# mLSTM heads: the denominator's squares bounded row by row, one column sum per token tile in place of two

## The chip, the cores and the metric

The kernel runs on one core of one Trainium2 chip. The metric is the device time of one execution in microseconds (us). Times in the profile are in us from the start of the profiled span, unless marked ns.

## The reference

The program is a two-layer streaming encoder on 512 tokens of width 1024 in float32. The change touches one part of layer 0: the four mLSTM heads of width 192 (DH).

```
num = sum_s s[t,s] v[s] + inter * q_t C          # per head, 192 values for each token
den = sum_s s[t,s]      + inter * q_t . n
h   = num / max(|den|, exp(-m_t))
h   = h * rsqrt(mean(h*h) + EPS)                  # over the 192 values of the head
out = h * head_g * sigmoid(o)                     # goes to the output projection
```

The division and the norm together are one factor for each token and head: `num * rsqrt(mean(num^2) + EPS * max(den^2, exp(-2 m)))`. Both kernels compute that factor.

## The kernel before, in words

**Layout.** Activations lie transposed: features on the 128 partitions, the 512 tokens along the free dimension. Most products are made of three single-precision products of rounded parts (`mm3`, lines 175 to 177: high x high, low x high, high x low), so each float32 operand is first split: ScalarE casts the high part (line 136), VectorE subtracts to get the low part (line 137). The weights take this path too (`wr` raw, `wh` high, `wl` low, three buffers each). The text calls one `mm3` of 512 columns a triple of filler.

**A head.** A head of 192 features fills one full tile (`full`) and half of a second (`sh`, rows `rs`). `mlstm_head` goes over four blocks of 128 source tokens: `weighted_scores` makes the decayed scores (a product with `sel` at line 1155 spreads a row of gates, ScalarE takes the exponential at line 1157, GpSimd masks it at line 1159, VectorE multiplies it with the scores at line 1168), and `products` multiplies them with the values into two accumulators, `nums`. The first accumulator holds 128 of the head's 192 numerators. The second holds the other 64 in half of its rows; in the other half the value matrix is all ones, so that all 64 rows hold the denominator.

**The end of a head.** ScalarE squares both accumulators (line 1195) and VectorE multiplies them into the output gate `og` (line 1197). For each of four tiles of 128 tokens TensorE then multiplies the squares, as the stationary operand, with a constant `mcf` of two columns (lines 1202 and 1203): column 0 gathers the numerators' sum of squares, column 1 the mean of the 64 denominator rows. On 128x4 values VectorE takes the maximum with `floor2`, which is exp(-2m) with tokens on the partitions (line 1207), scales it, adds the mean of squares, and takes an inverse square root by three Newton steps (lines 222 to 228). `diagonal` makes two diagonal matrices of the result (line 237), `spread` multiplies them with ones (line 250), so that each token's factor stands in all rows, and line 1216 multiplies `og` by it. The result is split and becomes an operand of the output projection.

**The gate work.** `gate_rows` computes the gates on four rows (one for each head) of 512 tokens. Its row `mr` is m, bounded at line 1086. Eight small transposes (lines 1096 and 1097) turn two rows into columns; of the second ScalarE takes exp(-2x) into `floor2` (line 1099).

**Order.** `weave(job, filler, each)` runs a job and takes `each` steps of filler at every `yield` of the job, or `each * n` at `yield n`; a filler step is mostly one `mm3` of a projection. In this part of the program a scheduler then orders the instructions of each engine by its own estimates and assigns the buffers; each engine executes its instructions in that order. Accumulators come in three kinds: `mm` (three banks), `sc` (three) and `tr` (two). The head's last factor is needed by the output projection: `outp.part(0, 4, 5)` and `outp.part(1, 4, 5)` follow the last head with no other work between.

Of the kernel before, what the change touches and what calls it, by code (L numbers as in the profile page):

```python
# [21 lines left out]
MEM = 256  # L22
AW = 768
AH = 4
DH = AW // AH
BH = 12
HD = 64
# [3 lines left out]
EPS = 1e-6  # L31
# [19 lines left out]
def f(ap):  # L51
    return ap.bitcast(F32)
# [3 lines left out]
def trunk(  # L56
# [18 lines left out]
    nc = tc.nc  # L75
    V, A, G = nc.vector, nc.scalar, nc.gpsimd

    cpool = ctx.enter_context(tc.tile_pool(name="cpool", bufs=1))
# [6 lines left out]
    dram = ctx.enter_context(tc.tile_pool(name="dram", bufs=1, space=bass.MemoryType.DRAM))  # L85

    def sb(tag, shape, dtype=F32):
        count[0] += 1
        return pool.tile(shape, dtype, tag=tag, name=f"{tag}{count[0]}", bufs=bufs[tag])

    def ps(tag):
        count[0] += 1
        return psum.tile([P, S], F32, tag=tag, name=f"p{tag}{count[0]}", bufs=pbufs[tag])

    def small(n=4):
        return sb("s", [P, 32])[:, :n]


    ident = cpool.tile([P, P], F32, name="ident")
    make_identity(nc, ident)  # L100
    ones = cpool.tile([P, P], F32, name="ones")
# [7 lines left out]
        out=maskf, in_=maskf, pattern=[[1, P]], base=0, channel_multiplier=-1,  # L109
# [8 lines left out]
            V.tensor_copy(sel[q], ident[q, 32 * s : 32 * s + AH].unsqueeze(2).to_broadcast([AH, AH, P]))  # L118
    eps = cpool.tile([P, 1], F32, name="eps")
    V.memset(eps, EPS)  # L120

    mcf = cpool.tile([P, 3, 2], F32, name="mcf")
    V.memset(mcf, 0.0)
    V.memset(mcf[:, 0, 0:1], 1.0)
    V.memset(mcf[:HD, 1, 0:1], 1.0)
    V.memset(mcf[HD:, 1, 1:2], 1.0 / HD)
    V.memset(mcf[:HD, 2, 1:2], 1.0 / HD)
    V.memset(mcf[HD:, 2, 0:1], 1.0)


    HEADS = (slice(0, HD), slice(HD, P))

# [86 lines left out]
    def rsqrt(y, v):  # L219
        n = v.shape[-1]  # L220
        yi = y.bitcast(I32)
        V.tensor_scalar(yi, v.bitcast(I32), 1, None, op0=ALU.logical_shift_right)
        V.tensor_scalar(yi, yi, -1, 0x5F3759DF, op0=ALU.mult, op1=ALU.add)
        t = small(n)
        for _ in range(3):
            V.tensor_mul(t, y, y)
            V.scalar_tensor_tensor(t, t, -0.5, v, op0=ALU.mult, op1=ALU.mult)
            V.scalar_tensor_tensor(y, t, 1.5, y, op0=ALU.add, op1=ALU.mult)
# [17 lines left out]
    def spread(dgs, tag):  # L246

        o = ps(tag)
        for i, dg in enumerate(dgs):
            nc.tensor.matmul(o, onesr, dg, start=i == 0, stop=i == 1)  # L250
        return o
# [176 lines left out]
    with tc.manual_schedule(engines={mybir.EngineType.PE, mybir.EngineType.Activation, mybir.EngineType.DVE}):  # L428
# [9 lines left out]
        for q in range(KT // 2 + 1):  # L438
            if q < KT // 2:
                tp = ps(("tr", "sc")[q % 2])  # L440
# [577 lines left out]
    e, u, c, r = (cpool.tile([P, TT, AH], F32, name=f"gate{i}") for i in range(4))  # L1018
    tot = cpool.tile([AH, 16], F32, name="tot")
    acol = cpool.tile([P, TT, AH], F32, name="acol")  # L1020
    floor2 = cpool.tile([P, TT, AH], F32, name="floor2")
    RO = [0, 512, 896, 1152, 1280]

    rp = []
# [1 line left out]
    def gate_rows():  # L1026

        V.tensor_copy(ic, gt[:, :, :AH])
        V.scalar_tensor_tensor(e, fg, -1.0, fg, op0=ALU.mult, op1=ALU.min)
        A.activation(e, e, AF.Exp)  # L1030
        V.tensor_scalar(u, e, 1.0, None, op0=ALU.add)
        A.activation(lf, u, AF.Ln)
        V.scalar_tensor_tensor(c, u, -1.0, e, op0=ALU.add, op1=ALU.subtract)
        V.reciprocal(r, u)
        yield
        pin(V.tensor_mul(c, c, r))
        V.tensor_tensor(out=lf, in0=lf, in1=c, op=ALU.subtract)
        V.scalar_tensor_tensor(lf, fg, 0.0, lf, op0=ALU.min, op1=ALU.subtract)
        yield
        yield  # L1040
        lfp, icp = ps("tr"), ps("tr")
        for T in range(TT):
            nc.tensor.transpose(lfp[:AH, T * P : (T + 1) * P], lf[:, T, :], ident)
            nc.tensor.transpose(icp[:AH, T * P : (T + 1) * P], ic[:, T, :], ident)
        yield
        lfr, br, ar, mr = (sb("t", [P, S])[:AH, :] for _ in range(4))
        rr = [sb("t", [P, S]) for _ in range(2)]
        rp.extend(sb("u", [P, S], F32R) for _ in range(2))
        for t in rp:
            G.memset(f(t), 0.0)  # L1050
        pin(V.tensor_copy(lfr, lfp[:AH, :]))
        yield
        for T in range(TT):
            sl = slice(T * P, (T + 1) * P)
            pin(V.tensor_tensor_scan(br[:, sl], ones[:AH, :], lfr[:, sl], 0.0, ALU.mult, ALU.add))
        yield
        pin(V.tensor_tensor(out=ar, in0=icp[:AH, :], in1=br, op=ALU.subtract))
        yield
        carry = 0.0
        for T in range(TT):  # L1060
            sl = slice(T * P, (T + 1) * P)
            pin(V.tensor_tensor_scan(mr[:, sl], ar[:, sl], ar[:, sl], carry, ALU.max, ALU.max))
            if T < TT - 1:
                e_ = (T + 1) * P - 1
                V.tensor_tensor(out=tot[:, T : T + 1], in0=mr[:, e_ : e_ + 1], in1=br[:, e_ : e_ + 1], op=ALU.add)
                carry = tot[:, T : T + 1]
            yield
        for s in range(TT):
            off = None
            for T in range(s, TT):  # L1070
                sl = slice(T * P, (T + 1) * P)
                dst = rr[s // 2][64 * (s % 2) : 64 * (s % 2) + AH, sl]
                if T == s:
                    pin(V.tensor_scalar(dst, mr[:, sl], -1.0, None, op0=ALU.mult))
                else:
                    end = br[:, T * P - 1 : T * P]
                    if off is None:
                        off = end
                    else:
                        k = 4 + 4 * s + T - s  # L1080
                        V.tensor_tensor(out=tot[:, k : k + 1], in0=off, in1=end, op=ALU.add)
                        off = tot[:, k : k + 1]
                    V.tensor_scalar(dst, mr[:, sl], -1.0, off, op0=ALU.mult, op1=ALU.add)
            yield
        pin(V.tensor_tensor(out=mr, in0=mr, in1=br, op=ALU.add))
        V.tensor_scalar(mr, mr, -40.0, None, op0=ALU.max)
        yield
        for s in range(TT):
            q, t = 64 * (s % 2), rp[s // 2]
            src, hi = rr[s // 2][q : q + AH, s * P :], t[q : q + AH, s * P :]  # L1090
            pin(V.tensor_copy(hi, src))
            V.tensor_tensor(out=t[q + 32 : q + 32 + AH, s * P :], in0=src, in1=f(hi), op=ALU.subtract)
            yield
        tp = ps("tr")
        for T in range(TT):
            nc.tensor.transpose(tp[:, T * AH : (T + 1) * AH], ar[:, T * P : (T + 1) * P], ident[:AH, :AH])
            nc.tensor.transpose(tp[:, 16 + T * AH : 16 + (T + 1) * AH], mr[:, T * P : (T + 1) * P], ident[:AH, :AH])
        pin(V.tensor_copy(acol, tp[:, :16].rearrange("p (t h) -> p t h", t=TT)))
        A.activation(floor2, tp[:, 16:32].rearrange("p (t h) -> p t h", t=TT), AF.Exp, scale=-2.0)

    mixes = [None] * KT

# [41 lines left out]
    def mlstm_head(h):  # L1144
        hp, odd = divmod(h, 2)
# [46 lines left out]
        sqs = []  # L1192
        for o, j, r in ((nums[0], full, slice(0, P)), (nums[1], sh, rs)):
            sq = sb("t", [P, S])
            A.activation(sq, o, AF.Square)
            sqs.append(sq)
            V.tensor_tensor(out=og[j][r, :], in0=o[r, :], in1=og[j][r, :], op=ALU.mult)
        yield
        st = ps("sc")
        for T in range(TT):  # L1200
            sl = slice(T * P, (T + 1) * P)
            nc.tensor.matmul(st[:, 2 * T : 2 * T + 2], sqs[0][:, sl], mcf[:, 0, :], start=True, stop=False)
            nc.tensor.matmul(st[:, 2 * T : 2 * T + 2], sqs[1][:, sl], mcf[:, 1 + odd, :], start=False, stop=True)
            yield 0.581
        st = st[:, : 2 * TT].rearrange("p (t c) -> p t c", c=2)
        z, fc = small(), small()
        V.tensor_tensor(out=z, in0=st[:, :, 1], in1=floor2[:, :, h], op=ALU.max)
        V.tensor_scalar(z, z, EPS, 1e-35, op0=ALU.mult, op1=ALU.max)
        V.scalar_tensor_tensor(z, st[:, :, 0], 1.0 / DH, z, op0=ALU.mult, op1=ALU.add)
        rsqrt(fc, z)  # L1210
        dg = diagonal(fc)
        yield 2.673
        fb = spread(dg, "sc")
        yield
        for j, r in ((full, slice(0, P)), (sh, rs)):
# [12 lines left out]
    fill = chain(a_tiles(2), a_memory_queries(0), a_tiles(3, 4), a_tiles(5), a_memory_queries(1))  # L1228
    memkv = load_memory_kv(0)
    weave(mlstm_head(0), fill, 1.4)  # L1230
    until(lambda: og[2] is not None, fill)
    weave(mlstm_head(1), fill, 1.125)
# [292 lines left out]
```

## Time and profile before

| what | value |
|---|---|
| time, median of 3 runs | 1197.71 us (1197.57 to 1198.04) |
| span of the profiled execution | 1197.4 us |
| TensorE products busy | 1186.5 us, 99% |
| TensorE weight loads busy | 1039.1 us, 87% |
| VectorE busy | 967.3 us, 81% |
| ScalarE busy | 718.4 us, 60% |
| GpSimd busy | 123.3 us, 10% |

The page gives the span of the profiled execution, 1197.4 us, and no time of its own around it; the median of the timed runs is 0.3 us above. In the rows, PE is TensorE, PEld its weight loads, DVE VectorE, ACT ScalarE, POOL GpSimd, SP SyncE. A row of the timeline reads: start, length, engine, line, operation, tile written from tiles read, shapes, number of merged instructions, and in brackets the idle time before it and what ended that. Products on TensorE are pipelined, so their lengths overlap: the distance of two starts is what a product costs. A float32 product (not split) is recorded as two passes.

### The profile page before, as it was taken

The page shows a single profiled execution, that of the slowest core. Times are in us where ns is not written, and L with a number is a line of the kernel's source. Part 1 is how long each engine was busy: PE and PEld are TensorE (multiplying, and loading weights), DVE is VectorE, ACT ScalarE, POOL GpSimd, SP SyncE. Part 2 cuts the span into 40 slices and gives each one's busy share as a digit, 9 for nine tenths or more (in the row PEclk, how much of TensorE's full clock was granted, in tenths as well). Part 3 has the DMA queues.
Part 4 walks back from the last instruction along what each step waited for, and adds up shares of the span by engine and source line. Part 5 has one row for each costly group of instructions (what it writes and reads, how often), then busy time and mean ns, then how long its engine had stood idle before and what let it go on. Part 6 is the DMA issues. An engine that isn't in the chain of part 4 may idle for free.

```text
span 1197.4 us, 18206 instructions
## 1 busy us (share of the span) xinstructions
PE 1186.5 (99%) x6735; PEld 1039.1 (87%) x6735; DVE 967.3 (81%) x1772; ACT 718.4 (60%) x1290; POOL 123.3 (10%) x206
## 2 busy tenths in 40 slices
PE   9999999999999999999999999999999999999997
PEld 8988888888889989999888888888889988999986
DVE  6778688878978888888698888997897888888855
ACT  5646577655655555555575667776565655555545
POOL 1200101000021111111021000001001011011100
PEclk9999999999999999999999999999999999999999
DMA  8634111454266666665563223146336466665551
GB/s 283 212 92 123 54 54 57 134 152 133 88 157 162 153 162 155 151 144 129 152 189 120 89 71 99 55 130 201 116 89 150 110 138 141 141 141 136 121 158 71
DMA packets 199131, 155.97 MB, mean 130 GB/s; under 512 B 7976, under 2 KB 179458, under 8 KB 199042
## 3 DMA queue, kind: packets, MB, share of 16 engines
q1 hardware_dynamic: 183906, 119.74, 34.2%
q0 software_dynamic: 14560, 34.02, 13.7%
q8 instruction: 53, 0.87, 0.3%
q10 hardware_dynamic: 576, 1.05, 0.2%
q14 instruction: 36, 0.29, 0.1%
HBM read 126.27 MB, written 32.44 MB: 133 GB/s over the span
## 4 chain that ended last, share of the span: by engine, by line
PE 93%; DMA 2%; ACT 2%; DVE 2%; issue 0%; SPq 0%; ACTq 0%; DVEq 0%
PE pmm L175 15%; PE pmm L176 15%; PE pmm L177 15%; PE ptr L175 6%; PE ptr L177 6%; PE ptr L176 6%; PE pmm L791 6%; PE psc L177 5%; PE psc L175 5%; PE psc L176 5%; PE pmm L790 3%; PE psc L525 2%; DMA wr<-in_mem_w_kv_dram 2%; PE ptr L1352 1%; PE ptr L1373 1%; PE ptr L1374 1%
## 5 line engine op out<-in xcount | busy, mean ns | idle before, releaser
L175 PE MATMUL pmm<-u,wh 128*128 128x512 f32 (+1 forms) x872 | 309.1, 355 | 0.3 <-ACT u L136 0.2
L176 PE MATMUL pmm<-u,wh 128*128 128x512 f32 (+1 forms) x872 | 306.3, 351 | 0.0
L177 PE MATMUL pmm<-u,wl 128*128 128x512 f32 (+1 forms) x872 | 306.3, 352 | 0.0
L137 DVE TENSOR_TENSOR wl<-wr,wh 128x1024 fp32r<-128x1024 f32 (+3 forms) x172 | 199.8, 1163 | 55.1 <-ACT wh L136 53.1
L136 ACT CAST wh<-wr 128x1024 fp32r<-128x1024 f32 (+3 forms) x172 | 172.1, 1002 | 99.8 <-PE pmm L176 45.2
L177 PEld LDWEIGHTS pmm<-u,wl 128*128 128x128 f32 x872 | 164.5, 189 | 20.9
L175 PEld LDWEIGHTS pmm<-u,wh 128*128 128x128 f32 x872 | 164.5, 189 | 18.7 <-ACT u L136 1.1
L176 PEld LDWEIGHTS pmm<-u,wh 128*128 128x128 f32 x872 | 164.7, 189 | 18.3 <-DVE u L137 0.5
L175 PE MATMUL ptr<-u,wh 128*128 128x512 f32 x272 | 106.7, 392 | 0.0
L177 PE MATMUL ptr<-u,wl 128*128 128x512 f32 x272 | 106.1, 390 | 0.0
L176 PE MATMUL ptr<-u,wh 128*128 128x512 f32 x272 | 105.9, 389 | 0.0
L759 POOL DMA_DIRECT2D xspill<-t x64 | 55.5, 867 | 462.5 <-ACT t L758 457.1
L136 ACT CAST u<-pt 128x512 fp32r<-128x512 f32 x102 | 62.8, 618 | 47.2 <-DVE pt L881 47.1
L137 DVE TENSOR_TENSOR u<-pt,u 128x512 fp32r<-128x512 f32 x102 | 69.9, 689 | 11.2 <-ACT u L136 8.5
L175 PE MATMUL psc<-u,wh 128*128 128x256 f32 (+1 forms) x232 | 76.1, 328 | 0.0
L177 PE MATMUL psc<-u,wl 128*128 128x256 f32 (+1 forms) x232 | 75.9, 327 | 0.0
L176 PE MATMUL psc<-u,wh 128*128 128x256 f32 (+1 forms) x232 | 75.9, 327 | 0.0
L791 PE MATMUL pmm<-u,u 128*128 128x512 f32 x192 | 69.6, 397 | 0.0
L943 ACT ACTIVATE t<-t 128x512 f32<-128x512 f32 x34 | 21.5, 632 | 79.4 <-DVE t L666 79.4
L827 DVE TENSOR_TENSOR t<-t,pmm 128x256 f32<-128x256 f32 x72 | 30.2, 420 | 45.0 <-ACT t L825 45.0
L758 ACT COPY t<-ptr 128x512 f32<-128x512 f32 x64 | 37.4, 584 | 42.8 <-PE ptr L177 42.8
L666 DVE SCALAR_TENSOR_TENSOR t<-t,cols,t 128x511 f32<-128x511 f32 x80 | 59.6, 746 | 3.7 <-ACT t L673 3.7
(305 smaller groups left out, 2671.5 us busy)
## 6 DMA issues: line engine op xcount, KB each, us to landing
wr<-in_ffn_w_up_dram SPq DMA_DIRECT2D x54, 512.0 KB, 4.5
wr<-in_ffn_w_down_dram SPq DMA_DIRECT2D x38, 512.0 KB, 4.1
pt<-in_ffn_w_up_dram SPq DMA_DIRECT2D x34, 512.0 KB, 6.0
xspill<-t POOLq DMA_DIRECT2D x64, 256.0 KB, 5.2
wr<-in_a_w_in_dram SPq DMA_DIRECT2D x20, 512.0 KB, 3.7
xspill<-u POOLq DMA_DIRECT2D x32, 256.0 KB, 2.7
u<-xspill SPq DMA_DIRECT2D x32, 256.0 KB, 5.1
wr<-in_w_kv_dram SPq DMA_DIRECT2D x12, 512.0 KB, 3.8
```

Of the source, the lines that this page charges most:

```text
L136: high = A.copy(hi, src) if on_act else V.tensor_copy(hi, src)
L137: low = V.tensor_tensor(out=lo, in0=src, in1=f(hi), op=ALU.subtract)
L175: nc.tensor.matmul(o, lh, rh, start=first, stop=False, skip_group_check=more)
L176: nc.tensor.matmul(o, lh, rl, start=False, stop=False, skip_group_check=more)
L177: nc.tensor.matmul(o, ll, rh, start=False, stop=last, skip_group_check=more)
L525: nc.tensor.matmul(o, a, b, start=first and i == 0, stop=i == 1)
L666: V.scalar_tensor_tensor(acc[:, n:], src[:, : S - n], self.fw[:, c * FT + j : c * FT + j + 1], acc[:, n:], op0=ALU.mult, op1=ALU.add,)
L758: A.copy(t, o)
L759: G.dma_start(xspill[j], t, accum_op=ALU.add)
L790: nc.tensor.matmul(r[:, :H], w[1][:, k], p[i - 1][:, :H], start=False, stop=False, skip_group_check=True)
L791: nc.tensor.matmul(r, w[0][:, k], p[i - 1], start=False, stop=k == n - 1, skip_group_check=True)
L827: V.tensor_tensor(out=o, in0=o, in1=r[:, H:], op=ALU.add)
```

## The change

The squares of the denominator are bounded where they lie. VectorE replaces the 64 denominator rows of the second tile of squares by max(den^2 * c, floor) with c = EPS * DH / HD, then adds the two tiles of squares. One float32 product for each tile of tokens, with a single column of ones, sums the 128 rows of the result: that is DH times what stands under the root. `mcf` and its memsets go, as do the second product, the maximum and the scaling behind the sums.

For this the floor is needed on 64 rows for each head, with tokens along the free dimension. `gate_rows` takes the exponential on the row `mr` itself, scales and bounds it, writes it to DRAM with one DMA and reads it back with four broadcasting DMAs, all on GpSimd's queue, into two tiles of the kind `bias`, one for each pair of heads. Four of the eight small transposes go. The yields around the sums change: 2.4 ahead of them and 3.4 behind them, in place of 0.581 after each pair and 2.673 behind.

```diff
-    mcf = cpool.tile([P, 3, 2], F32, name="mcf")
-    V.memset(mcf, 0.0)
-    ...
-    floor2 = cpool.tile([P, TT, AH], F32, name="floor2")
+    floor2 = dram.tile([AH, S], F32, name="floor2")
+    floors = []
...
         V.tensor_scalar(mr, mr, -40.0, None, op0=ALU.max)
+        A.activation(mr, mr, AF.Exp, scale=-2.0)
+        V.tensor_scalar(mr, mr, EPS * DH / HD, 1e-35, op0=ALU.mult, op1=ALU.max)
+        G.dma_start(floor2, mr)
+        for hp in range(2):
+            floors.append(sb("bias", [P, S]))
+            for odd, half in enumerate(reversed(HEADS)):
+                row = floor2[2 * hp + odd]
+                src = bass.AP(tensor=row.tensor, offset=row.offset, ap=[[0, HD], [1, S]])
+                G.dma_start(floors[hp][half, :], src)
         yield
...
-            nc.tensor.transpose(tp[:, 16 + T * AH : 16 + (T + 1) * AH], mr[:, T * P : (T + 1) * P], ident[:AH, :AH])
...
-        A.activation(floor2, tp[:, 16:32].rearrange("p (t h) -> p t h", t=TT), AF.Exp, scale=-2.0)
...
             V.tensor_tensor(out=og[j][r, :], in0=o[r, :], in1=og[j][r, :], op=ALU.mult)
+        dr = HEADS[1 - odd]
+        V.scalar_tensor_tensor(
+            sqs[1][dr, :], sqs[1][dr, :], EPS * DH / HD, floors[hp][dr, :], op0=ALU.mult, op1=ALU.max
+        )
+        V.tensor_add(sqs[0], sqs[0], sqs[1])
         yield
+        yield 2.4
         st = ps("sc")
         for T in range(TT):
-            sl = slice(T * P, (T + 1) * P)
-            nc.tensor.matmul(st[:, 2 * T : 2 * T + 2], sqs[0][:, sl], mcf[:, 0, :], start=True, stop=False)
-            nc.tensor.matmul(st[:, 2 * T : 2 * T + 2], sqs[1][:, sl], mcf[:, 1 + odd, :], start=False, stop=True)
-            yield 0.581
-        st = st[:, : 2 * TT].rearrange("p (t c) -> p t c", c=2)
+            nc.tensor.matmul(st[:, T : T + 1], sqs[0][:, T * P : (T + 1) * P], ones[:, :1], start=True, stop=True)
         z, fc = small(), small()
-        V.tensor_tensor(out=z, in0=st[:, :, 1], in1=floor2[:, :, h], op=ALU.max)
-        V.tensor_scalar(z, z, EPS, 1e-35, op0=ALU.mult, op1=ALU.max)
-        V.scalar_tensor_tensor(z, st[:, :, 0], 1.0 / DH, z, op0=ALU.mult, op1=ALU.add)
+        V.tensor_scalar(z, st[:, :TT], 1.0 / DH, None, op0=ALU.mult)
         rsqrt(fc, z)
         dg = diagonal(fc)
-        yield 2.673
+        yield 3.4
```

More of the change, by code (lines that the diff above doesn't have):

```diff
@@ L120, in trunk @@
     V.memset(eps, EPS)
-    mcf = cpool.tile([P, 3, 2], F32, name="mcf")
[L123 to L128, printed above, removed]
     HEADS = (slice(0, HD), slice(HD, P))
```

## The prediction

> **What bounds the kernel now.** I read the page first (busy time, the chain that ended last), then the waits of TensorE, then its timeline at each of the four mLSTM heads beside those of VectorE and ScalarE.
>
> ```profile
> PE 1186.5 (99%) x6735; PEld 1039.1 (87%) x6735; DVE 967.3 (81%) x1772; ACT 718.4 (60%) x1290; POOL 123.3 (10%) x206
> ...
> PE 93%; DMA 2%; ACT 2%; DVE 2%; issue 0%; SPq 0%; ACTq 0%; DVEq 0%
> ...
> PE pmm L434 <- DVE mcf L123: 1.1, 1, 1.1
> ```
>
> TensorE is busy 99% of the span and carries 93% of the chain; its longest wait is 1.1 us at the very start. Whatever TensorE no longer does, or newly waits for, moves the end one for one. The other engines count only through waits that they give TensorE.
>
> **What the sums cost TensorE.** Head 0, start times on TensorE (start, length, line):
>
> ```profile
> 125.38 0.28 PE L1202 MATMUL psc<-mcf,t 128*128 128x2 f32 x2
> 125.52 0.36 PE L1203 MATMUL psc<-mcf,t 128*128 128x2 f32 x2
> 125.74 0.47 PE L175 MATMUL pmm<-u,wh 128*128 128x512 f32 x1
> 126.06 0.39 PE L176 MATMUL pmm<-u,wh 128*128 128x512 f32 x1
> 126.29 0.40 PE L177 MATMUL pmm<-u,wl 128*128 128x512 f32 x1
> 126.52 0.28 PE L1202 MATMUL psc<-mcf,t 128*128 128x2 f32 x2
> ...
> 128.11 0.28 PE L1202 MATMUL psc<-mcf,t 128*128 128x2 f32 x2
> ...
> 98.51 0.20 PE L1097 MATMUL ptr<-ident,t 4*128 4x4 f32 x1
> 98.57 0.20 PE L1096 MATMUL ptr<-ident,t 4*128 4x4 f32 x1
> ```
>
> Starts are the measure, since lengths overlap. A filler product of 512 columns takes 0.23 (126.06 to 126.29), three of them, a triple, 0.69. From 125.38 to 126.52 lie one pair of sums and a triple: 1.14 - 0.69 = 0.45 for a pair, four passes. From 126.52 to 128.11 lie two pairs and a triple: 1.59 - 0.69 = 0.90, so a pair costs 0.45 in a row too. Half of it, 0.225, is one f32 product with a full stationary tile. A head has four pairs, 1.8; the change leaves four single products, 0.9. Four heads save 4 x 0.9 = 3.6. The four transposes of the floor (L1097) go as well, at 0.06 each: 0.24. Together -3.84 if nothing waits. One column or two is no matter: the passes are two columns wide now and cost 0.11, as long as their weight loads.
>
> **What is put in their way.** The squares no longer go straight from ScalarE to TensorE. VectorE must first do both multiplications of L1197 (in the program's order they stand ahead), then the bound (64x512) and the addition (128x512). Rows for these:
>
> ```profile
> 123.11 1.09 ACT L1195 ACTIVATE t<-ptr 128x512 f32<-128x512 f32 x2 [1.91 <-PE ptr L177]
> 123.73 1.28 DVE L1197 TENSOR_TENSOR u<-ptr,u 128x512 f32<-128x512 f32 x2 [1.82 <-ACT t L1195]
> 125.16 1.23 DVE L137 TENSOR_TENSOR wl<-wr,wh 128x1024 fp32r<-128x1024 f32 x1
> 95.68 1.40 DVE L507 SCALAR_TENSOR_TENSOR u<-t,u 64x512 fp32r<-64x512 f32 x2
> 261.27 0.69 DVE L270 TENSOR_TENSOR rb<-rb,t 128x512 f32<-128x512 f32 x1
> 129.38 0.16 DVE L1208 TENSOR_SCALAR s<-s 128x4 f32<-128x4 f32 x1
> 129.77 0.17 DVE L222 TENSOR_SCALAR s<-s 128x4 int32<-128x4 int32 x1
> ```
>
> The bound is priced as L507, 0.70, the addition as L270, 0.69. In the order that the changed program is built in, VectorE does L1197 twice, the bound, a weight subtraction (wl, 1.23) and only then the addition in heads 0, 1 and 3. The moved yields (2.4 ahead of the sums, 3.4 behind) ask for filler to cover this; what counts is the built order, and it gives TensorE six filler triples from the last product to the sums in head 0 (three before), 5.67 in head 1, 7.67 in head 2, 6.33 in head 3.
>
> Head 0: TensorE arrives three triples after 125.38, at 127.45. VectorE: L1197 to 125.01, bound to 125.7, wl to 126.85, addition to 127.45 and some. Wait 0.1.
>
> ```profile
> 150.45 0.28 PE L1202 MATMUL psc<-mcf,t 128*128 128x2 f32 x2
> 149.53 1.42 DVE L1197 TENSOR_TENSOR u<-ptr,u 128x512 f32<-128x512 f32 x2 [3.62 <-ACT t L1195]
> 151.50 1.22 DVE L137 TENSOR_TENSOR wl<-wr,wh 128x1024 fp32r<-128x1024 f32 x1 [0.56 <-ACT wh L136]
> 206.84 0.28 PE L1202 MATMUL psc<-mcf,t 128*128 128x2 f32 x2
> 208.33 0.73 DVE L1111 SCALAR_TENSOR_TENSOR t<-pmm,cols,t 128x509 f32<-128x509 f32 x1
> 215.60 0.50 PE L250 MATMUL psc<-t,onesr 128*128 128x512 f32 x1
> ```
>
> Head 1: arrival 150.45 plus 3.67 triples, 152.96; L1197 to 150.95, bound to 151.6, wl to 152.75, addition to 153.4: wait 0.45. Head 2: arrival 206.84 plus 4.67 triples, 210.05; the taps end at 209.06, bound 209.7, addition 210.4: wait 0.45 with the hand-over. After the sums the small steps lose two instructions (L1208, L1209: 129.38 to 129.77, 0.4), but a weight subtraction now stands inside them in heads 1 and 2, and fewer triples follow. By the same addition the spread product L250 waits 0.25 more in head 1; in head 2 a wait of 0.2 replaces one of about 0.2 (L250 is 0.50 long there). Head 3 is like head 1 or better. I take 0.3 for the three; ends: -0.4 x 3, the steps saved, if they had been waited for, and 1.2 x 3, a weight subtraction each.
>
> **Head 3 is the tight place.** There the filler runs out: the out projection's last products need this head.
>
> ```profile
> 244.61 0.28 PE L1202 MATMUL psc<-mcf,t 128*128 128x2 f32 x2
> 245.01 0.69 DVE L1197 TENSOR_TENSOR u<-ptr,u 64x512 f32<-64x512 f32 x1
> 245.73 0.96 DVE L137 TENSOR_TENSOR wl<-wr,wh 128x768 fp32r<-128x768 f32 x1
> 251.69 0.39 PE L176 MATMUL ptr<-u,wh 128*128 128x512 f32 x1
> 252.17 0.62 ACT L136 CAST wh<-wr 128x512 fp32r<-128x512 f32 x1 [6.75 <-PE ptr L176]
> 254.10 1.26 ACT L136 CAST u<-u 128x512 fp32r<-128x512 f32 x2
> 255.39 1.05 ACT L136 CAST wh<-wr 128x1024 fp32r<-128x1024 f32 x1
> 254.87 0.39 PE L177 MATMUL ptr<-u,wl 128*128 128x512 f32 x1
> 255.42 0.97 PE L175 MATMUL pmm<-u,wh 128*128 128x512 f32 x3 [0.16 <-ACT u L136]
> ```
>
> At 244.61 the changed order puts four triples ahead of the sums. The second accumulator of these takes the bank that L1197 reads until 245.70, and is reached at 245.30: wait 0.45 for the bank and its hand-over, to 245.75. Bound to 246.4, wl to 247.3, addition to 247.95; TensorE arrives ten products later, at 248.05, and waits 0.1 for the hand-over. The dear one comes last. The products at 255.42 need both casts of 254.10 (done 255.36): they wait 0.55 - 0.23 = 0.32 now, and 0.2 more in restarting. In the changed order the 1024-wide weight cast (255.39) stands between these two casts. It needs the buffer that the last filler triple still reads, and such a release takes from that product's end to 0.09 later (251.69 + 0.39 to 252.17). So the product that needs the second cast starts 0.39 + 0.09 + 1.05 + 0.63 + 0.06 (255.36 to 255.42) = 2.2 after the start of the last product that reads this buffer, where two products, 0.46, would do: wait 1.75. Less 0.52 now: +1.2. Between nothing (-0.5, if data came at once) and this I take this: every piece is in a row, and the order forces it.
>
> **The floor, and the two table loads.** The floor's exponential moves from the end of the gate work into it.
>
> ```profile
> 101.55 1.28 ACT L1099 ACT_TABLE_LOAD   x1
> 102.85 0.18 ACT L1099 ACTIVATE floor<-ptr 128x16 f32<-128x16 f32 x1
> 108.57 1.15 ACT L1157 ACTIVATE t<-psc,acol 128x512 f32<-128x512 f32 x2
> 109.38 0.72 POOL L1159 TENSOR_SCALAR_AFFINE_SELECT t<-t 128x128 f32<-128x128 f32 x2 [66.00 <-ACT t L1157]
> 110.30 1.14 DVE L1168 SCALAR_TENSOR_TENSOR t<-psc,t 128x512 f32<-128x512 f32 x2
> 111.17 0.28 PE L1155 MATMUL psc<-u,sel 128*128 128x256 f32 x1
> ```
>
> The load at 101.55 also served head 0's exponentials at 108.57. Now the gate work takes two loads, with convolution taps behind them. Their cover: three mm accumulators, so a tap may be late by a projection, 24 products of 0.23 or 5.5, before TensorE needs its bank; uncovered, 1.28 each. And head 0 pays its own load: first exponential at 109.85, select to 111.0, L1168 to 111.8. TensorE reaches the third L1155, which takes L1168's bank, at 111.4: wait 0.4; from 0, if the load slips into an idle stretch, to 1.3, the load itself. The next activation in the rows starts 1.30 after the load. The Trainium skill, "ScalarE: Activation LUTs", section "What ACT_TABLE_LOAD costs", gives 1283 ns and a drain of some 1380 ns for each switch; by that the first exponential, and the sum, would be 1.4 later again. The rows at 101.55 and 102.85 show no drain.
>
> GpSimd takes five more DMAs (one write, four broadcasts that wait for it). Behind them are two memsets and the selects; GpSimd idles 66 us before 109.38, so this is hidden; uncovered, the selects would move with it. The memsets of mcf go: the wait of 1.1 quoted first ends with one of them, but only warm-up products (L434, ones by ones) stand behind it: nothing. On SP one feed-forward weight load moves ahead of two out-projection loads; their cast, at 252.17, waited 6.75 for TensorE and not for data: nothing.
>
> **Sum.** -3.84 + 0.4 (load) + 0.1 + 0.45 + 0.45 + 0.55 (sums) + 0.3 (spreads) + 1.2 (tail) = -0.39; each new wait also slows the products after it by some 0.1 (the first of three at 255.42 takes about that extra), four times, +0.4. So 0.0 on a span of 1197.4; the median of 1197.71 lies 0.3 above the span. Forecast **1197.7 us**: the saved passes come back as waits. A difference below 0.2%, 2.4 us, is about what a measurement of this kernel cannot tell from no change. Own range of this case: nine waits, each off by some 0.2 and mostly by the same cause, 1.5 either way, 1196.2 to 1199.2. Chance 0.6.
>
> **Rivals.** (A) The cover holds: sums and spreads do not wait, and the load hides. What stays is at most the tail, whose cause is in the order itself: -3.84 to -2.6, so 1193.9 to 1195.1, say 1194.5. For it: 93% of the chain is TensorE's, so the orders of before hid such chains nearly everywhere. Against: by the rows above the additions end at or after TensorE's arrival in every head. Chance 0.2.
>
> (B) Slower: the weight subtraction between bound and addition (heads 0, 1, 3) holds VectorE. It waits for ScalarE's cast, which waits for a weight buffer that TensorE frees. In head 1 the cast ends 0.1 before the bound does; from the point where it ends later than the bound, every tenth goes straight into the sums' wait, up to one cast, 1.05, per head: 3 x 1.05 = 3.1, 1200.8. Against: in heads 0 and 3 the margin is 0.5 and 1.0. Chance 0.15.
>
> (C) The change does not save what it says: a single-column product that starts its own sum costs as much as the pair did, 0.45. Then 3.6 is missing: 1201.2. Against: two passes per product are in the rows. Chance 0.05.
>
> **Numbers.** Faster by over 0.2% (under 1195.3) is A: 0.2. Slower by over 0.2% (above 1200.1) is B and C: 0.2. Within: 0.6. Range 1194.5 to 1200.8: it leaves out half of A, C, and of B what is dearer than its price; under 2 in 10.
>
> **What would show it.** Right: four sums in a row 0.9 long per head; TensorE waits for VectorE's addition by 0.1 to 0.6; the widest gap, about 1.7, before the three L175 products at the end of head 3; the stages after it unchanged. Wrong: no gap at the sums (A), VectorE idle before wl between bound and addition (B), sums 1.8 long (C).

## The result, and the profile after

The changed kernel takes 1199.84 us (median of 19 runs, 1199.46 to 1201.63), the kernel before 1197.78 beside it (19 runs, 1197.55 to 1199.54). The ratio is 1.0017, 95% interval 1.0010 to 1.0023: 2.1 us slower, a little less than the 0.2% that the prediction took for measurable, but the interval leaves out 1. The forecast was 1197.7, no change. The saved passes were paid back and 2 us more with them. In every timed run whose span is on record the time lies some 1.7 us above it; the 0.3 that the prediction puts between span and median sets the span of one execution against the time of another. The difference of the two kernels does not hang on it.

The page of the changed kernel, its first line and the first line of its chain; then the longest waits of TensorE behind the first 45 us (in total, times, longest):

```profile
PE 1184.7 (99%) x6699; PEld 1034.4 (86%) x6699; DVE 971.5 (81%) x1767; ACT 720.5 (60%) x1290; POOL 124.4 (10%) x211
...
PE 90%; DVE 4%; ACT 3%; DMA 2%; issue 1%; SPq 0%; POOL 0%; DVEq 0%; ACTq 0%; POOLq 0%
...
PE pmm L166 <- ACT u L127: 1.6, 1, 1.6
PE psc L1206 <- DVE t L1201: 0.7, 2, 0.4
PE psc L516 <- ACT t L573: 0.4, 2, 0.2
PE ptr L167 <- DVE pt L128: 0.4, 1, 0.4
PE ptr L166 <- DVE u L1196: 0.3, 1, 0.3
```

TensorE has 36 instructions less and is busy 1.8 us less, yet its share of the chain falls from 93% to 90%, and VectorE's and ScalarE's grow. The first of these waits was 0.2 us before and is 1.6 now; the other four are not in the same view of the kernel before. These are the places on TensorE's timeline where it newly waits, but for one in memory attention 0 (start, length, line):

```profile
110.07 0.39 PE L166 MATMUL pmm<-u,wh 128*128 128x512 f32 x1
110.53 0.44 PE L166 MATMUL psc<-u,u 128*128 128x384 f32 x1
...
127.30 0.39 PE L168 MATMUL pmm<-u,wl 128*128 128x512 f32 x1
127.75 1.05 PE L1206 MATMUL psc<-ones,t 128*128 128x1 f32 x8
128.66 0.48 PE L166 MATMUL pmm<-u,wh 128*128 128x512 f32 x1
...
135.13 0.39 PE L167 MATMUL pmm<-u,wh 128*128 128x512 f32 x1
135.62 0.50 PE L241 MATMUL psc<-t,onesr 128*128 128x512 f32 x1
135.96 0.40 PE L1154 MATMUL psc<-u,sel 128*128 128x512 f32 x1
...
153.27 0.39 PE L167 MATMUL pmm<-u,wh 128*128 128x512 f32 x1
154.00 1.05 PE L1206 MATMUL psc<-ones,t 128*128 128x1 f32 x8 [0.34 <-DVE t L1201]
...
160.71 0.39 PE L166 MATMUL pmm<-u,wh 128*128 128x512 f32 x1
161.11 0.50 PE L241 MATMUL psc<-t,onesr 128*128 128x512 f32 x1
...
209.78 0.39 PE L167 MATMUL pmm<-u,wh 128*128 128x512 f32 x1
210.56 1.05 PE L1206 MATMUL psc<-ones,t 128*128 128x1 f32 x8 [0.39 <-DVE t L1201]
...
237.61 0.27 PE L168 MATMUL psc<-u,u 128*128 128x128 f32 x1
238.24 0.50 PE L167 MATMUL ptr<-pt,u 128*128 128x512 f32 x1 [0.35 <-DVE pt L128]
...
245.13 0.40 PE L168 MATMUL ptr<-u,wl 128*128 128x512 f32 x1
245.80 0.50 PE L166 MATMUL ptr<-u,wh 128*128 128x512 f32 x1 [0.27 <-DVE u L1196]
...
252.09 0.39 PE L168 MATMUL ptr<-u,wl 128*128 128x512 f32 x1
252.59 0.50 PE L241 MATMUL psc<-t,onesr 128*128 128x512 f32 x1
...
255.00 0.40 PE L168 MATMUL ptr<-u,wl 128*128 128x512 f32 x1
256.99 0.97 PE L166 MATMUL pmm<-u,wh 128*128 128x512 f32 x3 [1.58 <-ACT u L127]
```

A product of 512 columns starts 0.227 after the one ahead of it where nothing waits. What lies between two starts beyond that is the wait: 127.30 to 127.75 is 0.45, a wait of 0.225 in head 0; in the same way 0.504 in head 1 (153.27), 0.552 in head 2 (209.78), 0.444 for the bank in head 3 (245.13), 1.754 at the end of head 3 (255.00). The eight passes of the sums take 0.91 (127.75 to 128.66): the saving is there. After a wait the next product is late too (the restart of the prediction's sum): 135.62 to 135.96 is 0.34, 0.11 too much. Read like this over the whole trace, against 0.112 for each pass of a sum, 0.061 for a small transpose and, for products of other widths, the median distance of their kind, the waits of the two kernels stand so:

| stretch of the changed kernel's trace, us | waits before | waits after | new | what the prediction put there |
|---|---|---|---|---|
| 105 to 124.5, head 0 begins | 0.28 | 0.57 | 0.29 | 0.4 |
| 124.5 to 136.3, head 0's sums, spread | 0.09 | 0.77 | 0.68 | 0.1 |
| 149 to 162, head 1's sums, spread | 0.16 | 1.02 | 0.86 | 0.45, and 0.3 for the spreads of heads 1 to 3 |
| 162 to 204, memory attention 0 | 0.79 | 0.97 | 0.18 | 0 |
| 204 to 217.2, head 2's sums, spread | 0.45 | 0.93 | 0.48 | 0.45 |
| 217.2 to 243, memory attention 1, head 3's scores | 0.89 | 1.35 | 0.46 | 0 |
| 243 to 254, head 3's sums, spread | 0.13 | 1.11 | 0.98 | 0.55 |
| 254 to 260, its end | 0.57 | 2.12 | 1.55 | 1.2 |
| all else | 14.91 | 15.17 | 0.26 | 0 |
| restarts (in the rows above where measured) | | | | 0.4 |
| sum | 18.27 | 24.01 | 5.74 | 3.85 |

Saved: 32 passes of 0.112 and four transposes of 0.061, 3.83. New waits less this are 1.91; the spans are 1199.3 and 1197.4. That the account closes follows from how it is made, since a wait is whatever lies beyond these fixed prices; what it tells is where the time stands.

Behind the waits stand VectorE in head 1, and ScalarE at the end of head 3, first VectorE's rows, then ScalarE's:

```profile
150.08 1.42 DVE L1196 TENSOR_TENSOR u<-ptr,u 128x512 f32<-128x512 f32 x2 [3.80 <-ACT t L1194]
151.53 0.69 DVE L1198 SCALAR_TENSOR_TENSOR t<-t,bias 64x512 f32<-64x512 f32 x1
152.13 1.21 DVE L128 TENSOR_TENSOR wl<-wr,wh 128x1024 fp32r<-128x1024 f32 x1
153.27 0.68 DVE L1201 TENSOR_TENSOR t<-t,t 128x512 f32<-128x512 f32 x1
```

```profile
254.54 0.62 ACT L127 CAST u<-u 128x512 fp32r<-128x512 f32 x1 [0.96 <-DVE u L1215]
255.25 1.05 ACT L127 CAST wh<-wr 128x1024 fp32r<-128x1024 f32 x1
256.32 0.62 ACT L127 CAST u<-u 64x512 fp32r<-64x512 f32 x1
```

The bound took 0.69 and the addition 0.68, the weight subtraction between them 1.21, and the sums start 0.05 after the addition ends. At the end the 1024-wide weight cast stands between the two casts, and the products at 256.99 start when the second is done (256.94).

### The profile page after: what moved, and what is told of

Same layout as the page of the kernel before. It is cut to its first block, busy times and chain, and to the rows that moved or that the text cites. A ratio compares the mean times of both kernels' runs of the same rounds, so it can differ in the third digit from the quotient of the medians.

```text
span 1199.3 us, 18137 instructions
## 1 busy us (share of the span) xinstructions
PE 1184.7 (99%) x6699; PEld 1034.4 (86%) x6699; DVE 971.5 (81%) x1767; ACT 720.5 (60%) x1290; POOL 124.4 (10%) x211
## 3 DMA queue, kind: packets, MB, share of 16 engines
q10 hardware_dynamic: 576, 1.05, 0.2%
## 4 chain that ended last, share of the span: by engine, by line
PE 90%; DVE 4%; ACT 3%; DMA 2%; issue 1%; SPq 0%; POOL 0%; DVEq 0%; ACTq 0%; POOLq 0%
PE pmm L166 14%; PE pmm L167 14%; PE pmm L168 14%; PE ptr L166 6%; PE ptr L167 6%; PE pmm L782 6%; PE ptr L168 6%; PE psc L168 5%; PE psc L166 5%; PE psc L167 5%; PE pmm L781 3%; PE psc L516 2%; DMA wr<-in_mem_w_kv_dram 2%; PE ptr L1351 1%; PE ptr L1372 1%
```

## The experiments

Each kernel was timed beside the kernel before. Ratios are to that kernel, with their 95% intervals. The last column but one works the time out from one trace alone: new waits (and slow passes) after the first 52 us, against the kernel before, less the passes saved. The first 52 us are left out: the waits there add up to 3.5 to 5.8 us over the traces, and differ by 0.9 between the two traces of e4's kernel (an e-number stands for each kernel in the text).

| | kernel | median, us | ratio, interval | by its trace, us | measured, us |
|---|---|---|---|---|---|
| | the change | 1199.84 | 1.0017 (1.0010 to 1.0023) | 5.70 - 3.83 = +1.9 | +2.0 |
| e1 | before, one product of each pair | 1194.92 | 0.9974 (0.9965 to 0.9983) | 0.27 - 3.58 = -3.3 | -3.1 |
| e2 | change, no bound, no addition | 1197.21 | 0.9988 (0.9979 to 0.9997) | 1.93 - 3.83 = -1.9 | -1.4 |
| e3 | change, end of head 3 turned | 1198.58 | 1.0006 (0.9997 to 1.0015) | 3.75 - 3.83 = -0.1 | +0.7 |
| e4 | change, bound and addition early | 1196.61 | 0.9988 (0.9979 to 0.9997) | 2.08 - 3.83 = -1.8 | -1.4 |
| e4 | the same again | 1196.14 | 0.9985 (0.9976 to 0.9994) | 2.03 - 3.83 = -1.8 | -1.8 |
| e5 | change, floor later | 1200.27 | 1.0014 (1.0005 to 1.0023) | 5.62 - 3.83 = +1.8 | +1.7 |
| e6 | e4, floor later, other yields | 1197.44 | 0.9997 (0.9988 to 1.0006) | 3.10 - 3.83 = -0.7 | -0.4 |
| e7 | before, end of head 3 turned | 1197.39 | 0.9999 (0.9990 to 1.0008) | -0.35 | -0.1 |
| e8 | before, the change's yields | 1201.36 | 1.0021 (1.0011 to 1.0031) | +1.9 | +2.5 |
| e9 | change, two root steps | 1199.61 | 1.0014 (1.0006 to 1.0023) | 5.30 - 3.83 = +1.5 | +1.7 |
| e10 | change, addition on GpSimd | 1203.84 | 1.0051 (1.0039 to 1.0064) | 9.74 - 3.83 = +5.9 | +6.1 |
| e11 | e4, addition on GpSimd | 1199.20 | 1.0011 (1.0002 to 1.0020) | 5.87 - 3.83 = +2.0 | +1.3 |

Trace and time agree within 0.8 everywhere, and each figure from a trace lies inside the interval of its ratio: the waits account for the times as closely as these runs can tell.

**e1, is the saving real?**

```
 nc.tensor.matmul(st[:, 2 * T : 2 * T + 2], sqs[0][:, sl], mcf[:, 0, :], start=True, stop=False)   # stop=True
-nc.tensor.matmul(st[:, 2 * T : 2 * T + 2], sqs[1][:, sl], mcf[:, 1 + odd, :], start=False, stop=True)
```

> The kernel before, with the second product of each pair of sums left out (16 products of one head size less; the share of the second tile of squares, and with it the denominator, is missing from the output). Nothing else moves: the squares still go straight from ScalarE to TensorE. Theory W (the saving is real and waits eat it): TensorE does 16 x 0.225 = 3.6 less work and waits for nothing new, so 3.6 us less than the kernel before, 3.0 to 3.8 if a few of its present waits grow. Theory C (the products that are left get dearer, or a saved pass is not saved time): 0 to 1 us less, and sums that stand more than 0.9 us long per head.

Measured: 3.1 us less. A saved pass is saved time, and the kernel before has room for it. Theory C falls.

**e2, without VectorE's two steps.**

```
-V.scalar_tensor_tensor(sqs[1][dr, :], sqs[1][dr, :], EPS * DH / HD, floors[hp][dr, :], op0=ALU.mult, op1=ALU.max)
-V.tensor_add(sqs[0], sqs[0], sqs[1])
```

> The changed kernel without the bound and without the addition: four products over the first tile of squares alone, so the denominator is missing from the output. The saved passes and the whole floor (exponential in the gate work, table loads, five DMAs) stay. Theory W (the loss is in the waits for the two VectorE steps): the waits at the sums (2.0 us with restarts), at the spread products (1.2) and at the end of head 3 (1.85, because the casts there come in the kernel's old order again) mostly vanish: 4 to 5 us less than the changed kernel, 1194.5 to 1195.8. Theory F (the loss is in the floor and its table loads, spread over many small waits): at most 1.5 us less than the changed kernel, above 1198.

Measured: 0.0029 of 1197.8, 3.5 us, less than the change. No sum waits in any head, nor do the spread products of heads 0 and 1, and the wait at the end of head 3 falls from 1.754 to 0.544. But the time is 1.7 above e1's, which saves as many passes without the new yields and without the floor: head 3's bank still waits 0.445, its spread 0.277, head 2's 0.333, memory attention 0 0.239. Theory W holds for most of it and was too high by half a microsecond and more, since these waits do not come from the two steps.

**e3, the end of head 3.**

```
-for j, r in ((full, slice(0, P)), (sh, rs)):
+for j, r in ((sh, rs), (full, slice(0, P))) if h == 3 else ((full, slice(0, P)), (sh, rs)):
```

> The changed kernel, with the order of the last two multiplications and splits turned round in head 3 alone, so that the two half-tile and full-tile casts are both issued ahead of or close by the 1024-wide weight cast instead of one on each side of it in the changed kernel's order; no work is added or taken. Theory W: the wait of 1.75 us ahead of the three L166 products at the end of head 3 falls to between 0.1 and 0.6, the time by 1.1 to 1.6 us against the changed kernel; the other waits stay. Theory D (VectorE is simply later by 1.4 us per head and the tail shows it whatever the order): the wait moves to the other tile's product and keeps at least 1.2; the time changes by less than 0.4.

Measured: 1.3 less than the change by the two ratios, and TensorE at the end of head 3 does not wait at all. Its rows, then ScalarE's:

```profile
253.37 0.40 PE L168 MATMUL ptr<-u,wl 128*128 128x512 f32 x1
253.60 0.94 PE L166 MATMUL pmm<-u,wh 128*128 128x512 f32 x3
...
252.91 0.62 ACT L127 CAST u<-u 64x512 fp32r<-64x512 f32 x1 [0.96 <-DVE u L1215]
253.61 1.05 ACT L127 CAST wh<-wr 128x1024 fp32r<-128x1024 f32 x1
254.56 0.62 ACT L127 CAST u<-u 128x512 fp32r<-128x512 f32 x1
```

The wait of 1.754 is gone, with no work taken away: it came from the order of the casts. Theory D falls. But the order is not the one that was expected, since the weight cast still stands between the other two. What the turn changed is which of them is ahead of it. The three products need the half tile, for in both kernels they start within 0.07 of the end of its cast (256.94 in the change, 253.53 here); in the program the full tile's products come behind them, and here three more products of this kind start at 255.85, after the full tile's cast has ended (255.18).

**e4, bound and addition written ahead of the output gate's multiplications.**

```
+V.scalar_tensor_tensor(sqs[1][dr, :], ..., floors[hp][dr, :], op0=ALU.mult, op1=ALU.max)
+V.tensor_add(sqs[0], sqs[0], sqs[1])
 for o, j, r in ((nums[0], full, slice(0, P)), (nums[1], sh, rs)):
     V.tensor_tensor(out=og[j][r, :], in0=o[r, :], in1=og[j][r, :], op=ALU.mult)
```

> The changed kernel, with the bound and the addition put ahead of the two multiplications of the output gate (L1196) on VectorE; the same instructions, so the same busy time on every engine. Theory W (what counts is when the sums' operand is ready): the sums' waits (0.225, 0.504, 0.552 and the bank's 0.444) shrink to at most 0.2 each except where the accumulators' banks are now freed later (head 3's may grow to 1 or so), the spread's waits shrink with them, and at the tail the weight cast stands behind both casts again, so the wait of 1.75 goes to about 0.3: 2.5 to 4 us less than the changed kernel, 1196 to 1197.3. Theory D (VectorE's extra 1.4 us per head is what costs): within 1 us of the changed kernel.

Measured: 0.9988 and, again, 0.9985: 3.5 and 3.8 us less than the change with the same instructions. In the order that was built VectorE does not do as the program says, but near to it. Head 0:

```profile
123.83 0.69 DVE L1202 TENSOR_TENSOR u<-ptr,u 128x512 f32<-128x512 f32 x1 [1.81 <-ACT t L1194]
124.56 0.69 DVE L1197 SCALAR_TENSOR_TENSOR t<-t,bias 64x512 f32<-64x512 f32 x1
125.28 0.68 DVE L1202 TENSOR_TENSOR u<-ptr,u 64x512 f32<-64x512 f32 x1
125.88 0.67 DVE L1200 TENSOR_TENSOR t<-t,t 128x512 f32<-128x512 f32 x1
...
127.14 1.21 DVE L128 TENSOR_TENSOR wl<-wr,wh 128x1024 fp32r<-128x1024 f32 x1
```

The bound fills the place between the two multiplications, and the weight subtraction stands behind the addition, which ends at 126.55 where the change ended it at 127.70. Heads 0, 1 and 3 do not wait for their sums; head 2 still does, by 0.64, since three convolution taps are woven between the steps. The casts at the end of head 3 come in the old order, and the wait there goes to 0.26. e4 with both steps is as fast as e2 without them (0.9988 and 0.9985 against 0.9988): well placed they cost nothing that these runs can tell. Theory D falls here as well.

> The kernel with the bound and the addition ahead of the output gate's multiplications once more, unchanged, on the same chip as the others of this call, to settle whether it is faster than the kernel before by more than 0.2%: 1196.1 to 1197.0 and a ratio of 0.998 to 0.9995 by its first run.

It came out at the low end of this, below 1 in its whole interval both times. e4 is faster than both kernels.

**e5, the floor at the end of the gate work.** The nine lines from the exponential to the last DMA moved behind the copy to `acol`, the exponential kept in program order.

> The changed kernel, with the floor's exponential, its scaling and its five DMAs moved to the end of the gate work, so that head 0's first exponential finds its table loaded again; the sums and all else stay. Theory W: the wait at 110.07 (0.235 and 0.107 of restart) and the head of it in ScalarE go, 0.3 us less than the changed kernel, 0 to 0.5. Theory F (the floor's share is the larger part of the loss, through the table loads and the DMAs in the gate work): 1 us less or more. Theory L (the floors now land too late for head 0's bound): head 0's sums wait longer by up to 2 us.

The wait at 110.07 stayed (0.228 and 0.107), and so did the time. ScalarE's rows tell why:

```profile
86.74 1.28 ACT L1090 ACT_TABLE_LOAD   x1
...
89.15 1.28 ACT L1111 ACT_TABLE_LOAD   x1 [0.48 <-DVE t L1110]
...
109.12 1.28 ACT L1156 ACT_TABLE_LOAD   x1
```

In the program the exponential now stands behind transposes that run at 99.10, but in the order that was built it moved by only 1.6 us (from 86.47 in the change to 88.03, behind the load at 86.74). It still lies ahead of convolution tiles, which load their own table at 89.15. The edit did not do what it was for; whether head 0's load costs 0.3 stays untested. That the floor as a whole is not the loss is shown by e4, which keeps it.

**e6, e4 with e5 and other yields (ahead of the sums 2.4 in all in heads 0 to 2 and 1.5 in head 3, in place of 3.4; behind them 4.4 in place of 3.4).**

> A version meant to be faster than both: the changed kernel with the bound and the addition ahead of the two multiplications of the output gate, with the floor at the end of the gate work, and with a triple of filler less ahead of the sums and one more behind them in heads 0 and 1. Theory W: against the kernel with only the first of these, the load's wait (0.34) goes and the spread products' waits of heads 0 and 1 (0.27 and 0.15, with 0.1 of restart each) go if the sums do not wait in turn: 1195.5 to 1196.1, 1.9 to 2.5 us less than the kernel before. Theory D (VectorE's added work costs wherever it stands): the sums of heads 0 and 1 wait by as much as the spreads no longer do, 1196.3 or more.

Worse than e4 by 0.9 to 1.2 ratio points in a thousand: one triple less ahead of the sums, and head 1 waits 0.500 where e4 did not wait at all; head 0's spread still waits 0.285, head 1's 0.177, and memory attention 0 waits 0.378 in a place where e4 has no wait. Theory D's number, but not its mechanism: the addition was where it had been, TensorE came earlier.

**e7, e3's turn in the kernel before.**

> The kernel before, with the last two multiplications and splits turned round in head 3 alone. Theory W: the wait of 0.32 and 0.2 of restarts ahead of the three L175 products at the end of head 3 shrinks, 0.3 to 0.5 us less than the kernel before. So little would also show that the turn in the changed kernel won its 1.3 us by undoing what the change had done to the order of the casts and not by a gain open to any version. If it wins over 1 us here too, that reading is wrong.

0.1 us less, within the interval of nothing; the trace has 0.35 of waits less in all. A small gain at most, so e3 won its 1.3 by undoing what the change had done there.

**e8, the change's yields alone.**

```
+yield 2.4
 st = ps("sc")
 ...
-    yield 0.581        # between the pairs of sums
...
-yield 2.673
+yield 3.4
```

> The kernel before, with the changed kernel's yields around the sums (2.4 ahead, none between, 3.4 behind) and nothing else of the change: the pairs of sums stand in one block after 18, 15, 18 and 12 products, and no bound, addition or floor is added, no pass saved. Theory W (the rearranged order has a price of its own, which the prediction put at 0.45 for the bank in head 3 and next to nothing for the spreads): the bank wait of 0.45 shows in head 3 and the spread products wait 0.1 to 0.3 in two or three heads: 0.5 to 1.5 us more than the kernel before. Theory V (all the new waits are VectorE's two added steps): within 0.3 us of the kernel before, no gap at the spreads or at the bank.

Measured: 2.5 us slower, above what either theory said. Theory V falls; W had the places (bank 0.457, spreads 0.127, 0.152 and 0.255) and missed the largest: memory attention 0, far from the edit, waits 1.0 more, 0.589 of it in one place that had no such wait before.

**e9, a shorter chain behind the sums.**

```
-rsqrt(fc, z)      # three steps
+rsqrt(fc, z, 2)
```

> The changed kernel with two steps of the reciprocal square root in the mLSTM heads instead of three (the factor is a little less exact; three small VectorE instructions less per head between the sums and the spread products). In the order that it is built in, each head has two products less between sums and first spread, and at the end of head 3 both casts come ahead of the 1024-wide weight cast again. Theory P (the planner that places the products takes the chain from the sums to the spread for shorter than it is, and so the spread waits wherever the chain ends): the spreads still wait 0.2 to 0.3 in heads 0, 1 and 3, and only the tail's wait goes, from 1.75 to 0.3 to 0.6: 1.2 to 1.5 us less than the changed kernel. Theory S (the spreads wait because the chain behind the sums is too long): their waits and restarts go too, 2.2 to 2.7 us less.

Neither theory came out. The spreads wait 0.11 in heads 0 and 3 and not in 1 and 2, as S says; the end of head 3 waits 0.265, as both say; 2 us were won at these places. The time is 0.3 less than the change's. The rest went here:

```profile
183.22 0.34 PE L1154 MATMUL psc<-u,sel 128*128 128x384 f32 x1
184.23 0.66 PE L585 MATMUL ptr<-ident,t 128*128 128x128 f32 x4 [0.67 <-DVE pt L128]
185.49 0.72 PE L599 MATMUL ptr<-pt,u 128*128 128x512 f32 x2 [0.60 <-DVE pt L128]
```

Memory attention 0 now waits 0.835 and 0.762 for VectorE, where the change waits for neither. Six small instructions fewer ahead of it, and another order is built, in which convolution taps of 0.74 stand among the subtractions that these products wait for.

**e10 and e11, the addition on GpSimd** (`G.tensor_add` for `V.tensor_add`; e10 in the change, e11 in e4).

> The changed kernel with the addition of the two tiles of squares on GpSimd instead of VectorE; the bound stays on VectorE. In heads 0, 1 and 3 the weight subtraction then stands behind the bound but no longer ahead of the addition, and the tail's casts come in the kernel's old order. GpSimd is nearly idle; what an addition of 128x512 takes there no row shows (a memset of 64x512 takes 0.55 us, so I reckon 0.7 to 2). Theory W (the operand's readiness is all): if it takes up to 1.0, the sums' waits go (1.3 with restarts in heads 0 to 2), the tail's 1.4 too: 2.5 to 3.5 us less than the changed kernel; if it takes 2, the sums wait 0.5 to 1 in each head and the gain is 0 to 1. Theory D (VectorE's load is what costs): the gain is there, 2 us or more, even where the sums wait longer.

> The kernel with the bound and the addition ahead of the output gate's multiplications, and the addition on GpSimd as well. Theory W: as with the addition on GpSimd alone, but the bound is ready 0.7 us earlier in heads 0, 1 and 3, so a slow addition (up to 1.5) is hidden too: 1195.0 to 1196.5. If the addition takes 2 or more, above 1197.

e10 is 4.1 us slower than the change, e11 about 3 slower than e4. GpSimd's four additions in e10:

```profile
124.71 2.25 POOL L1201 TENSOR_TENSOR t<-t,t 128x512 f32<-128x512 f32 x1 [8.88 <-ACT t L1107]
...
151.42 2.12 POOL L1201 TENSOR_TENSOR t<-t,t 128x512 f32<-128x512 f32 x1 [7.86 <-DVE t L1198]
...
210.33 1.26 POOL L1201 TENSOR_TENSOR t<-t,t 128x512 f32<-128x512 f32 x1 [11.41 <-ACT t L1111]
...
248.28 1.84 POOL L1201 TENSOR_TENSOR t<-t,t 128x512 f32<-128x512 f32 x1 [8.30 <-DVE t L1198]
```

The sums wait 0.762, 1.486, 1.458 and 1.439 for them. Theory W's dear case, and dearer than its price, for reasons that no theory had (see the last section). Theory D's gain is not there.

## Why the prediction was right or wrong

**Saved passes: right.** 0.91 for the four sums of a head against 0.9, and 3.83 in all against 3.84; e1 takes 3.58 of them alone and gains 3.1 (2.0 to 4.2). The passes start 0.11 apart, and so do their weight loads; each load is 0.19 long, so "as long as" in the prediction holds for their distance. Rival C is out.

**The sums' waits: right, and the total better than its parts.** 0.504, 0.552 and the bank's 0.444 against 0.45 each; in head 0 0.225 against 0.1, and in head 3 none for the addition (247.97 to 248.21) against 0.1. With restarts the four heads' stretches, without the spreads, have 1.95 new; the terms were 0.1, 0.45, 0.45, 0.55 and 0.4, the same. The place between bound and addition was read rightly from the built order. Rival B, that the subtraction itself would come late, did not occur: it starts 0.6 after the bound does, with no idle time ahead of it (151.53, 152.13).

**The end of head 3: right in its path.** A wait of 1.754 against 1.75. The weight cast starts 0.08 after the last product that reads its buffer has ended (254.78, 0.39 long), and the products that need the second cast start 2.21 after that product does, 2.2 forecast; e3 shows that the order of the casts is the cause. (The full tile's cast ends at 255.16, with that product, so the trace does not tell which of the two held the weight cast back.) The stretch has 1.55 more where 1.2 stood: the prediction took off the 0.2 of restarts that the kernel before has there, and they stayed.

**The spread products: the term that was mis-sized.** 0.3 was put for heads 1 to 3, 0.25 of it for head 1, and head 0 was left out. Head 1 came near, with 0.179 and 0.114 and the weight subtraction among the small steps (158.36), as forecast; head 2 has nothing new. Head 0 has 0.258 and 0.111. There the bound and the addition push a convolution tap of 0.74 from ahead of the sums to behind them: two taps (128.92, 129.69) stand among the small steps, where the kernel before has one (128.72) and e2, which does not wait there, has one too (128.59). Head 3, taken to be like head 1 or better, has 0.274 and 0.109, and there the two steps are not the cause: e2 without them waits 0.277, and e8 with the yields alone 0.255. Together these are 1.05, 0.75 too little. e9, with a third of the root's steps cut, leaves 0.11 and 0.12 of the waits of 0.258 and 0.274 and next to nothing of head 1's.

**"The stages after it unchanged": wrong.** This is the mechanism that the prediction lacked: an edit in a head changes the order that is built beyond it. 0.18 and 0.46 came up in the two memory attentions and head 3's scores, 0.26 in small waits elsewhere, and all were put at nothing. The prediction priced VectorE's lateness and took the new order itself for free but for one bank. e8 prices the yields in the kernel before: 2.5 us (1.3 to 3.7), before any step is added. It is another order than the change's, so its price is not a term of the change's sum; it shows the size. The same holds for e9's 1.6 in one stage. Nor are the yields the whole of it in the change: its longest wait in these stages, 0.518 at 237.61, is missing in e8, which has the yields alone, and in e2, e4 and e9, which have the yields and the floor; e3, e5 and e10 have it. Which instruction brings it stays open.

Together these are 0.75, 0.9 and 0.35, less 0.1 at the first load: the 1.9 that the forecast of no change missed. The load's price (0.34 against 0.4) was near. The Trainium skill's drain behind a table load ("ScalarE: Activation LUTs", section "What ACT_TABLE_LOAD costs") is not in the rows of the changed kernel either: where the activation waits for nothing else, it stands 1.3 behind the start of the load (108.49, 109.79).

**Rival A** came closest to what the change could have been. With the same instructions in another order (e4) the time is 1.4 to 1.8 under the kernel before: its condition, that the sums be covered, is a matter of where two instructions of 0.69 stand. It does not reach the rival's 1194.5, because the sums of head 2, the bank in head 3, three spreads and the first load still wait.

## What to carry to other kernels

On an engine that is busy 99%, count the saved passes in full, and then follow the operand of the moved products through the order as it is built, down to which long instruction got between two short ones: here a 1.2 us subtraction between bound and addition, and a 1.05 us cast ahead of the one that the next products needed, took back more than half of 3.8 us. A change in how much filler stands ahead of a step reorders stages far behind it, and here cost 2.5 us by itself where the step saves 3.8; time the new order alone, without the new work, to tell them apart. When a profile shows such a loss, first move instructions in program order: it gave 3.5 us here for no work taken away.

## What the runs showed of the hardware

**Twice a wait of over a microsecond was followed by half the clock.** In e10 the products of 512 columns start 0.43 apart from 252.4 to 255.4, two microseconds after the sums of head 3 had waited 1.4 us, and a window of that kernel shows the granted clock (the figure behind the busy times):

```profile
252.20:255.30 3.10, 3.10 (x9) 2.43 (x8) 2.71 (x12) 0.00 (x0) 0.00 (x0) 0.51 0.02 7
```

0.51 for 3.1 us, which costs 1.6 more on top of the wait. e11 shows the same from 211 to 214.3 (0.51) after a wait of 1.07. The changed kernel's own wait, 1.75 at 255.0, was followed by no such drop (1.00 from 255 to 263), nor were two of 1.46 and 1.49 in e10. The other twelve traces have the full clock from 8 to 1189 us. Which waits are followed by a drop, and whether the wait is the cause, stays open. The Trainium skill ("TensorE: Matmul & The Clock Gate", section "What's actually happening") has half rate after an idle window of some 3.4 us, in windows that run free of the kernel: the half rate and the length agree with these rows, the idle time that it needs does not, since TensorE idled for half of that at most.

**GpSimd's addition took 1.26 to 2.90 us** for 128x512, where VectorE takes 0.69. Two of VectorE's rows in e10 beside the four of GpSimd above:

```profile
124.59 1.23 DVE L128 TENSOR_TENSOR wl<-wr,wh 128x1024 fp32r<-128x1024 f32 x1
...
210.87 1.27 DVE L128 TENSOR_TENSOR u<-t,u 128x512 fp32r<-128x512 f32 x1 [0.69 <-ACT u L127]
```

The addition at 124.71 ends at 126.96, 1.14 after the subtraction that began 0.12 ahead of it (125.82). The one at 210.33 began first and took 1.26; VectorE's subtraction at 210.87, 0.69 elsewhere, took 1.27 and ended 0.55 after it. In these two they take turns, and the one that began first goes first. It is not always so: in e11 the addition that began at 124.28 took 2.90 and ended 1.13 after a weight subtraction (124.84, 1.21 long) that had begun 0.56 behind it. Nor does every instruction of VectorE take part: two convolution taps, which read an accumulator, took 1.53 beside the first of these additions (125.73) and 1.53 with none beside them (126.30 in the kernel before). The Trainium skill ("Trainium Architecture — The Big Picture", section "What this means for kernel authors") has the port pair that VectorE and GpSimd share as an exclusive lock and no split of bandwidth: the two rows of e10 agree.

**A wait costs TensorE another 0.1 us** in the product that follows the first one after it (0.34 for 0.227, at 135.62), whatever its length: 0.108 behind a wait of 0.04 (e9, 159.22) and behind one of 1.754. Behind the sums it is otherwise: there the second product is 0.09 late with a wait ahead of the sums (154.91) and without one (249.01).
